# Stick-breaking attention on eight cores: one stream per slot, or one stream per operation with rings between them, and the last projection begun inside the last head

## The chip, the cores and the metric

The kernel runs on the 8 cores of one Trainium2 chip; each core works on one batch element, and no core talks to another. The metric is device time in microseconds (us) of the slowest core. Most executions of one kernel agree within about 0.3%, except for a second, slower state in which one die or both have a lower granted TensorE clock.

Engines are named as in the profile: PE is TensorE, DVE is VectorE, ACT is ScalarE, POOL is GpSimd, SP is SyncE (here it only issues DMAs). An engine runs its instructions in the order in which the program lists them (in the trace of the changed kernel POOL's 384 differences and SP's 256 transposes keep it).

## The reference

The model has one mLSTM layer and one stick-breaking attention layer, both with a projection in, a projection out and a LayerNorm. The change touches the second layer only:

```python
def _stick_breaking(q, k, v):                      # q,k,v: [B,16 heads,2048,128]
    ...
    for blk in range(s // QBLOCK):                 # blocks of 128 queries
        z = einsum(qb, kp) * scale                 # [.., 128, t1], keys up to t1
        mask = key < query
        log_1mb = where(mask, log_sigmoid(-z), 0)
        between = cumsum(log_1mb, reverse=True) - log_1mb
        a = where(mask, exp(log_sigmoid(z) + between), 0)
        outs.append(einsum(a, vp))

def _stick_breaking_layer(x, k_sh, v_sh, w_in, w_out, ln_g, ln_b):
    u = x @ w_in;  q, z = split(u)                 # k_sh, v_sh = split(x @ kv_w)
    att = _stick_breaking(q, k_sh, v_sh)
    y = (att * silu(z)) @ w_out
    return layernorm(ALPHA * x + y, ln_g, ln_b)
```

The kernel computes the running product R of sigmoid(-z) with a scan from the last key to the first; the attention weights are the differences of neighbouring values of R.

## The kernel before

The program is built by a small scheduler. Each activity is a Python generator that yields operations; the scheduler keeps an estimated time for each engine and each buffer, always takes the operation that could start first by that estimate, and so fixes the order of every engine's instructions when the program is built. I call these estimates its **beliefs**. On the chip, semaphores keep the results right whatever the real times are, but the order can't change any more.

```python
    def dma(self, q, slot, out, in_, R=(), W=(), A=(), cost=4.0, **kw):
        ...
        start = self.est(q, list(R) + list(A), W)
        ...
        self.t[q] = start + (1.0 if q == "pool" else 0.1)
        self.tdma = max(self.tdma, start) + cost      # ONE line of DMA work for all queues
        self._time(self.tdma + 2.0, R, W)             # believed landing
```

For each of 16 heads, 4 projections (K, Q, V and the gate; 64 matmuls of 512 columns each; each has 0.5 MB of weights, which come from HBM by POOL's queue into one of four buffers) run beside 16 query blocks of attention. One block was one sequential stream, and two such streams ran side by side:

```python
            def tblock(k, slot):
                ...
                chunks = [(0, n)] if n <= 8 else [(8, n), (0, 8)]       # n key blocks of 128
                for ci, (b0, b1) in enumerate(chunks):
                    yield lambda: any(zfree)                            # one of two PSUM regions of 1024
                    ... matmuls Q.K -> PZ[zi]                           # PE   "scores"
                    ... sigmoid(-scale * PZ[zi]) in place               # ACT
                    ... tensor_tensor_scan -> RR[slot]                  # DVE  "scan"
                    ... AA[slot] = RR shifted - RR                      # POOL "difference"
                yield DMA transpose AA[slot] -> TT[gi][:, 0:n, block j] # SP   "transpose"
            def av():  # per group of four blocks: TT[gi] x V -> PSUM, times gate, to DRAM "midd"
            ...
            Sched(kb).run([av(), counted(0), counted(1), loads(), proj()])
            kb.barrier()
            ... ln_epilogue(...)   # load midd, 16 tiles: 64 matmuls each, residual, LayerNorm, store
```

Of the kernel before, what the change touches and what calls it, by code (L numbers as in the profile page):

```python
# [15 lines left out]
KC = 16  # L16
# [9 lines left out]
class KB:  # L26
# [4 lines left out]
    def __init__(self, nc, es):  # L31
        self.nc = nc
        self.es = es
        self.eng = {"pe": nc.tensor, "act": nc.scalar, "dve": nc.vector, "pool": nc.gpsimd, "sp": nc.sync}
        self.sem = {e: es.enter_context(nc.semaphore("s_" + e)) for e in ("pe", "act", "dve", "pool")}
        self.cnt = {e: 0 for e in self.sem}
        self.seen = {e: {} for e in self.eng}
        self.lastw = {}
        self.reads = {}
        self.pend = {e: ([], []) for e in self.eng}  # L40
        self.dsem = {}
        self.semobj = dict(self.sem)
        self.t = {e: 0.0 for e in self.eng}
        self.tdma = 0.0
        self.tw = {}
        self.tr = {}
# [45 lines left out]
    def est(self, e, R, W):  # L92
        R, W = self._norm(R, W)
        t = self.t[e]
        for k in R:
            t = max(t, self.tw.get(k, 0.0))
        for k in W:
            t = max(t, self.tw.get(k, 0.0), self.tr.get(k, 0.0))
        return t

    def _time(self, end, R, W):
        for k in R:
            self.tr[k] = max(self.tr.get(k, 0.0), end)
        for k in W:
            self.tw[k] = end

    def op(self, e, fn, R=(), W=(), inc=True, cost=0.3):
# [12 lines left out]
        self._time(start + cost + self.LAT[e], R, W)  # L120
# [12 lines left out]
    def dma(self, q, slot, out, in_, R=(), W=(), A=(), cost=4.0, **kw):  # L133
# [8 lines left out]
        self.tdma = max(self.tdma, start) + cost  # L142
        self._time(self.tdma + 2.0, R, W)
# [25 lines left out]
class Sched:  # L169
# [6 lines left out]
    def run(self, streams):  # L176
        live = [[g, None] for g in streams]
        while live:
            best, bt = None, None
            for s in live:  # L180
                while s[1] is None:
                    try:
# [14 lines left out]
                t = self.kb.est(o.e, o.R, o.W)  # L197
                if o.slack and t > self.kb.t[o.e]:
                    t += o.slack
                if bt is None or t < bt - 1e-9:  # L200
                    best, bt = s, t
            ended = any(s[0] is None for s in live)
# [17 lines left out]
def build():  # L220
# [20 lines left out]
    with contextlib.ExitStack() as es:  # L241
# [3 lines left out]
        WB = [sb(f"WB{i}", [128, KC, 128], BF16) for i in range(2)]  # L245
# [603 lines left out]
        def phase_b(x_src, dst, SRC, skey):  # L849
# [4 lines left out]
            WS = WB + [sa(f"WBx{i}", [128, KC, 128], BF16) for i in range(2)]  # L854
            QTs = [sa(f"QTb{i}", [128, S], BF16) for i in range(2)]
            KTs = [sa(f"KTb{i}", [128, S], BF16) for i in range(2)]
            VVs = [sa(f"VVb{i}", [128, NT, 128], BF16) for i in range(2)]
            SZs = [sa(f"SZb{i}", [128, S], F32) for i in range(2)]
            VT = sa("VTb", [128, S], BF16)
            TZ = [sa(f"TZ{i}", [128, 512], F32) for i in range(2)]  # L860
            AA = [sa(f"AA{i}", [128, S], BF16) for i in range(2)]
            TT = [sa(f"TT{i}", [128, NT, 512], BF16) for i in range(2)]
            ST = [sa(f"ST{i}", [128, 512], BF16) for i in range(2)]
            MK = sa("MK", [128, 2048], BF16)
# [3 lines left out]
            kb.op("dve", lambda: V.memset(MK[:, 0:1920], 0.0), W=["MK"])  # L868
            kb.op("dve", lambda: V.tensor_scalar(out=MK[:, 1920:2048], in0=MASKL[:], scalar1=1.0, scalar2=None,
                                                 op0=ALU.mult), R=["MASKL"], W=["MK"])  # L870
            for i in range(2):
                kb.op("dve", lambda: V.memset(RR[i][:, 2048:2056], 1.0), W=[f"SCR{i}"])

            st = {"heads": -1, "tb": -1, "av": -1, "uload": 0, "uused": 0, "z": 0}
            zfree = [True, True]
            rfree = [True, True]
            PZ = [PSA[:, 0:1024], PSA[:, 1024:2048]]
            zkeys = [[("ps", 0), ("ps", 1)], [("ps", 2), ("ps", 3)]]
            BAV = [4, 5]
            BPJ = [6, 7]  # L880

# [4 lines left out]
            def loads():  # L886
                for i, (w, u) in enumerate(units):
                    while st["uused"] < i - 3:
                        yield lambda i=i: st["uused"] >= i - 3
                    yield Op("pool", None, W=[f"WB{i % 4}"], cost=5.0,  # L890
                             dma=dict(slot=f"wb{i % 4}", out=WS[i % 4][:], in_=w[u]))
                    st["uload"] = i + 1

            def proj():
                nbk = 0
                for i in range(len(units)):
                    h, kind = i // 4, i % 4
                    par = h % 2
                    if kind == 0:
                        yield lambda h=h: st["heads"] >= h - 2  # L900
                    yield lambda i=i: st["uload"] > i
                    for tb in range(4):
                        bank = BPJ[nbk % 2]
                        nbk += 1
                        tsl = slice(tb * 512, (tb + 1) * 512)
                        for c in range(KC):
                            yield Op("pe", lambda c=c, bank=bank, i=i, tsl=tsl: P_.matmul(  # L907
                                PS[bank], lhsT=WS[i % 4][:, c, :], rhs=SRC[:, c, tsl], start=(c == 0),
                                stop=(c == KC - 1)), R=[f"WB{i % 4}", skey], W=[("ps", bank)], inc=(c == KC - 1),
                                cost=0.216)  # L910
                        if kind == 3:
                            zi = nbk % 2
                            yield Op("act", lambda bank=bank, zi=zi: A_.activation(out=TZ[zi][:], in_=PS[bank],
                                                                                   func=AF.Sigmoid),
                                     R=[("ps", bank)], W=[f"TZ{zi}"], cost=0.65)
                            yield Op("dve", lambda bank=bank, zi=zi, tsl=tsl, par=par: V.tensor_tensor(
                                out=SZs[par][:, tsl], in0=PS[bank], in1=TZ[zi][:], op=ALU.mult),
                                R=[("ps", bank), f"TZ{zi}"], W=[("SZ", par, tb)], cost=0.7)
                        else:
                            dstT, key = ((KTs[par], ("KT", par)), (QTs[par], ("QT", par)), (VT, "VT"))[kind]  # L920
                            yield Op("act", lambda dstT=dstT, bank=bank, tsl=tsl: A_.copy(out=dstT[:, tsl],
                                                                                          in_=PS[bank]),
                                     R=[("ps", bank)], W=[key], cost=0.65)
                    st["uused"] = i + 1
                    if kind == 2:
                        yield Op("sp", None, R=["VT"], W=[("VV", par)], cost=2.5,
                                 dma=dict(slot=f"vv{par}", out=VVs[par][:], in_=VT[:], transpose=True))
                    if kind == 3:
                        st["proj"] = h
                for nb in range(4):  # L930
                    yield Op("pool", None, W=[skey], cost=11.0,
                             dma=dict(slot=f"wo{nb}", out=SRC[:, :, nb * 512:(nb + 1) * 512], in_=b_w_out[nb]))

            st["proj"] = -1
            blocks = [(h, gq, j) for h in range(NH_B) for gq in range(4) for j in range(4)]

            def tblock(k, slot):
                h, gq, j = blocks[k]
                par, gi = h % 2, (4 * h + gq) % 2
                tb = 4 * gq + j  # L940
                n = tb + 1
                off = S - 128 * n
                yield lambda: st["proj"] >= h
                yield lambda: st["av"] >= 4 * h + gq - 2
                chunks = [(0, n)] if n <= 8 else [(8, n), (0, 8)]
                for ci, (b0, b1) in enumerate(chunks):
                    w = (b1 - b0) * 128
                    zi = []
                    yield lambda: any(zfree)
                    zi = zfree.index(True)  # L950
                    zfree[zi] = False
                    for o in range(0, w, 512):
                        ww = min(512, w - o)
                        yield Op("pe", lambda zi=zi, o=o, ww=ww, b0=b0: P_.matmul(  # L954
                            PZ[zi][:, o:o + ww], lhsT=QTs[par][:, tb * 128:(tb + 1) * 128],
                            rhs=KTs[par][:, b0 * 128 + o:b0 * 128 + o + ww], start=True, stop=True),
                            R=[("KT", par), ("QT", par)], W=[zkeys[zi][o // 512]], cost=max(ww, 128) / 2400 + 0.01,
                            slack=0.5)
                    zk = zkeys[zi][:(w + 511) // 512]
                    yield Op("act", lambda zi=zi, w=w: A_.activation(out=PZ[zi][:, 0:w], in_=PZ[zi][:, 0:w],  # L960
                                                                     func=AF.Sigmoid, scale=-scale),
                             R=zk, W=zk, cost=0.2 + w * 0.000833)
                    mk = MK[:, 2048 - w:2048] if ci == 0 else MK[:, 0:w]
# [107 lines left out]
```

## Time and profile before

Median 3506 us; the traced execution took 3498.88 us, its slowest core 3497.3 us. The timeline has three stages: the mLSTM layer to 1548 us, the heads to 3225, the last projection with LayerNorm to 3497.

The view of windows gives the busy time of each engine in a stretch. After the stretch and its length come PE, PEld (weight loads), DVE, ACT and POOL, each with the number of instructions, then the granted TensorE clock (1.00 is full speed), the busy share of the DMA engines and GB/s. Before, slowest core:

```profile
2900.00:3000.00 100.00, 80.37 (x344) 33.72 (x343) 44.83 (x33) 28.03 (x42) 36.50 (x30) 0.91 0.47 77
3088.00:3225.00 137.00, 28.95 (x81) 8.47 (x79) 43.00 (x29) 18.48 (x26) 37.82 (x28) 0.55 0.63 98
3225.00:3245.00 20.00, 0.00 (x0) 0.00 (x0) 0.00 (x0) 1.12 (x1) 0.00 (x0) 0.50 0.89 280
3245.00:3497.00 252.00, 224.38 (x1024) 99.61 (x1024) 149.49 (x176) 6.49 (x32) 72.10 (x16) 0.97 0.44 153
```

In the heads (first row) no engine is full, and 80.37 overstates PE: a matmul that stands alone is shown with its whole latency, about 0.4 us, while 128 projection matmuls in a row take 27.8 us (0.217 us each). The last head (second row) is nearly a hole.

The view of waits, before, from the second to the fifteenth head (columns: who waited, for whom, us in total, times, longest):

```profile
POOL WBx L146 <- PE PSA L907: 210.1, 13, 17.0
PE PSA L954 <- DVE SCR L966: 134.0, 155, 3.2
POOL AA L971 <- DMA TT<-AA: 128.8, 61, 3.7
PE PSA L994 <- DMA TT<-AA: 127.2, 40, 5.2
```

L954 is scores, L966 scan, L971 difference, L994 AV. PE waits for scans and for transposes: 261 us in 13 heads, 20 us a head. POOL's wait in the first line is for a weight buffer that PE still reads.

The chain of waits in the last head, before (start, length, what): POOL's in-order queue stands behind the loads of the output weights (in the program all four loads write one key, so each waits until the one before has landed).

```profile
3088.80 17.53 DMA HT<-b_w_out
3106.99 17.75 DMA HT<-b_w_out
3125.38 18.96 DMA HT<-b_w_out
```

### The profile page before, as it was taken

The page shows a single profiled execution, that of the slowest core. Times are in us where ns is not written, and L with a number is a line of the kernel's source. Part 1 is how long each engine was busy: PE and PEld are TensorE (multiplying, and loading weights), DVE is VectorE, ACT ScalarE, POOL GpSimd, SP SyncE. Part 2 cuts the span into 40 slices and gives each one's busy share as a digit, 9 for nine tenths or more (in the row PEclk, how much of TensorE's full clock was granted, in tenths as well). Part 3 has the DMA queues.
Part 4 walks back from the last instruction along what each step waited for, and adds up shares of the span by engine and source line. Part 5 has one row for each costly group of instructions (what it writes and reads, how often), then busy time and mean ns, then how long its engine had stood idle before and what let it go on. Part 6 is the DMA issues. An engine that isn't in the chain of part 4 may idle for free.

```text
span 3497.3 us, 38611 instructions; the slowest of 8 cores (3480.0 to 3497.3 us)
## 1 busy us (share of the span) xinstructions
PE 2819.5 (81%) x13444; PEld 1285.7 (37%) x13444; DVE 1606.0 (46%) x2768; ACT 1084.5 (31%) x2016; POOL 923.8 (26%) x732
## 2 busy tenths in 40 slices
PE   5899999999999869978878877887877877832897
PEld 4344444444444324433333333333333333310343
DVE  2354454544544355533444444544444444513465
ACT  2253453544535422222222222322222222301000
POOL 0021220211212212222333333333333333313233
PEclk9999999999999969989999999999999999965999
DMA  8121202202112163333544444444444444364453
GB/s 228 21 37 19 37 13 49 37 13 43 33 23 37 23 146 128 138 98 67 77 75 81 79 74 83 79 71 80 82 73 80 78 78 81 70 95 96 166 184 131
DMA packets 387053, 271.09 MB, mean 78 GB/s; under 512 B 326864, under 2 KB 359728, under 8 KB 376112
## 3 DMA queue, kind: packets, MB, share of 16 engines
q1 hardware_dynamic: 349856, 184.65, 21.7%
q0 software_dynamic: 37008, 83.96, 15.3%
q8 instruction: 113, 1.85, 0.2%
q14 instruction: 76, 0.62, 0.1%
HBM read 230.88 MB, written 41.94 MB: 78 GB/s over the span
## 4 chain that ended last, share of the span: by engine, by line
PE 55%; DVE 14%; DMA 14%; POOL 6%; issue 5%; ACT 4%; SPq 1%; DVEq 0%; POOLq 0%; ACTq 0%
PE PSA L907 13%; PE PSA L651 12%; PE PSA L372 9%; DVE SCR L966 9%; DMA TT<-AA 8%; PE PSA L314 6%; PE PSA L548 6%; POOL AA L971 4%; PE PSA L994 3%; PE PSA L954 2%; DMA XT<-a_w_out 2%; ACT PSA L960 2%; DMA HT<-b_w_out 2%; POOL SCR L393 1%; DMA HT<-x 1%
## 5 line engine op out<-in xcount | busy, mean ns | idle before, releaser
L971 POOL TENSOR_TENSOR AA<-SCR 128x1024 bf16<-128x1024 f32 (+7 forms) x384 | 530.8, 1390 | 506.3 <-DVE SCR L966 332.2
L907 PE MATMUL PSA<-HT,WB 128*128 128x512 bf16 x2048 | 555.7, 399 | 8.8 <-DMA WB<-kv_w 8.8
L907 PE MATMUL PSA<-HT,WBx 128*128 128x512 bf16 x2048 | 505.1, 390 | 0.0
L651 PE MATMUL PSA<-XT,GW 128*128 128x512 bf16 x2048 | 477.2, 392 | 0.0
L960 ACT ACTIVATE PSA<-PSA 128x1024 f32<-128x1024 f32 (+7 forms) x384 | 287.6, 759 | 592.4 <-PE PSA L954 590.7
L966 DVE TENSOR_TENSOR_SCAN SCR<-PSA,MK 128x128 f32<-128x128 f32 (+7 forms) x256 | 340.1, 1348 | 236.0 <-ACT PSA L960 148.6
L994 PE MATMUL PSA<-TT,VVb 128*128 128x512 bf16 (+3 forms) x640 | 248.0, 397 | 180.7 <-DMA TT<-AA 179.8
L954 PE MATMUL PSA<-KTb,QTb 128*128 128x512 bf16 (+3 forms) x640 | 195.2, 373 | 230.3 <-DVE SCR L966 230.1
L966 DVE TENSOR_TENSOR_SCAN SCR<-PSA,SCR,MK 128x1024 f32<-128x1024 f32 x128 | 298.7, 2342 | 146.2 <-POOL AA L971 76.2
L907 PEld LDWEIGHTS PSA<-HT,WB 128*128 128x128 bf16 x2048 | 205.6, 102 | 250.2 <-issue 55.3
L907 PEld LDWEIGHTS PSA<-HT,WBx 128*128 128x128 bf16 x2048 | 204.5, 100 | 252.0 <-issue 28.0
L651 PEld LDWEIGHTS PSA<-XT,GW 128*128 128x128 bf16 x2048 | 205.6, 101 | 240.9 <-issue 29.2
L393 POOL TENSOR_TENSOR SCR<-SCR,LNG 128x2048 f32<-128x2048 f32 x32 | 144.2, 4508 | 412.8 <-DVE SCR L390 412.8
L372 PE MATMUL PSA<-HT,MG 128*128 128x512 bf16 x1024 | 224.4, 381 | 31.9 <-DMA MG<-midd 23.0
L548 PE MATMUL PSA<-XT,WB 128*128 128x512 bf16 x1024 | 235.0, 382 | 2.4 <-ACT DB L502 2.4
L372 PE MATMUL PSA<-XT,HT 128*128 128x512 bf16 x1024 | 225.4, 381 | 4.7 <-DMA XT<-a_w_out 4.7
L314 PE MATMUL PSA<-XT,WB 128*128 128x512 bf16 x1024 | 222.3, 379 | 0.0
L1000 DVE TENSOR_TENSOR ST<-PSA,SZb 128x512 bf16<-128x512 f32 x64 | 43.8, 685 | 342.6 <-PE PSA L994 342.6
L669 POOL TENSOR_TENSOR SCR<-SCR 128x512 f32<-128x512 f32 x64 | 81.0, 1265 | 416.7 <-ACT SCR L667 416.7
L954 PEld LDWEIGHTS PSA<-KTb,QTb 128*128 128x128 bf16 x640 | 54.3, 99 | 360.4 <-issue 337.4
L994 PEld LDWEIGHTS PSA<-TT,VVb 128*128 128x128 bf16 x640 | 68.3, 107 | 287.4 <-issue 241.7
L725 DVE SCALAR_TENSOR_TENSOR STM<-PSA,WW,MASKC 128x128 bf16<-128x128 f32 x128 | 44.9, 351 | 247.7 <-PE PSA L723 225.6
(145 smaller groups left out, 2846.8 us busy)
## 6 DMA issues: line engine op xcount, KB each, us to landing
y<-SCR SPq DMA_DIRECT2D x32, 1024.0 KB, 3.9
SCR<-x SPq DMA_DIRECT2D x24, 1024.0 KB, 5.2
WB<-a_w_in POOLq DMA_DIRECT2D x32, 512.0 KB, 5.2
GW<-a_w_in POOLq DMA_DIRECT2D x32, 512.0 KB, 11.5
SCR<-y SPq DMA_DIRECT2D x16, 1024.0 KB, 5.9
HT<-x SPq DMA_DIRECT2D x8, 1024.0 KB, 10.3
XT<-a_w_out POOLq DMA_DIRECT2D x4, 2048.0 KB, 15.2
WB<-kv_w POOLq DMA_DIRECT2D x16, 512.0 KB, 6.2
```

The costliest lines, as they stand in the source:

```text
L314: kb.op("pe", lambda: P_.matmul(PS[bank][:, :], lhsT=WB[u.slot][:, c, :], rhs=src[:, c, tb * 512:(tb + 1) * 512], start=(c == 0), stop=(c ...
L372: kb.op("pe", lambda: P_.matmul(PS[bank][:, :], lhsT=midf(c, t), rhs=wo_buf[:, c, nb * 512:(nb + 1) * 512], start=(c == 0), stop=(c == KC ...
L393: kb.op("pool", lambda: G.tensor_tensor(out=full, in0=full, in1=LNG[:], op=ALU.mult), R=[sk, "LNG"], W=[sk])
L548: kb.op("pe", lambda: P_.matmul(PS[bank][:, :], lhsT=WB[u.slot][:, c, :], rhs=XT[:, c, tb * 512:(tb + 1) * 512], start=(c == 0), stop=(c = ...
L651: kb.op("pe", lambda: P_.matmul(PS[gb_][:, :], lhsT=gw[:, c, :], rhs=XT[:, c, tb * 512:(tb + 1) * 512], start=(c == 0), stop=(c == KC - 1) ...
L669: kb.op("pool", lambda: G.tensor_tensor(out=GO[pp], in0=GO[pp], in1=GWf[pp], op=ALU.add), R=[ko, kw] + gco[pp] + gcw[pp], W=[ko])
L907: yield Op("pe", lambda c=c, bank=bank, i=i, tsl=tsl: P_.matmul(PS[bank], lhsT=WS[i % 4][:, c, :], rhs=SRC[:, c, tsl], start=(c == 0), sto ...
L954: yield Op("pe", lambda zi=zi, o=o, ww=ww, b0=b0: P_.matmul(PZ[zi][:, o:o + ww], lhsT=QTs[par][:, tb * 128:(tb + 1) * 128], rhs=KTs[par][: ...
L960: yield Op("act", lambda zi=zi, w=w: A_.activation(out=PZ[zi][:, 0:w], in_=PZ[zi][:, 0:w], func=AF.Sigmoid, scale=-scale), R=zk, W=zk, cos ...
L966: yield Op("dve", lambda zi=zi, w=w, mk=mk, lo=lo, hi=hi, init=init: V.tensor_tensor_scan(out=RR[slot][:, lo:hi][:, ::-1], data0=PZ[zi][:, ...
L971: yield Op("pool", lambda lo=lo, hi=hi, b0=b0, b1=b1: G.tensor_tensor(out=AA[slot][:, b0 * 128:b1 * 128], in0=RR[slot][:, lo + 1:hi + 1], ...
L994: yield Op("pe", lambda sb_=sb_, f0=f0, bank=bank, par=par, gi=gi, nb_=nb_: P_.matmul(PS[bank][:, f0:512], lhsT=VVs[par][:, sb_, :], rhs=T ...
```

## The change

The intent: no engine should wait for the latency of a single block. Every operation gets a stream of its own, with rings between: five PSUM banks of 512 columns for scores, a ring of 32 key blocks for differences, V transposed in quarters, output weights loaded per column block, and the last projection is a stream that may start while the last head still runs. The core of the diff (cut):

```diff
-        self.tdma = 0.0
+        self.tdma = {}
 ...
-        self.tdma = max(self.tdma, start) + cost
-        self._time(self.tdma + 2.0, R, W)
+        self.tdma[q] = max(self.tdma.get(q, 0.0), start) + cost
+        self._time(self.tdma[q] + 2.5, R, W)
 ...
-            def tblock(k, slot):  ... scores, sigmoid, scan, difference, transpose in one stream
+            def zs():             # for every block, chunks of 512 from the diagonal down
+                        bank = zfree.pop(0)
+                        ... matmul -> PS[bank]; sigmoid in place; zq.append((k, ci, bank))
+            def scan():           # cost=0.12 + w * 0.0022
+                        ... scan PS[bank] -> RR[slot]; zfree.append(bank); sq.append((k, ci))
+            def sub():            # ring AA of 32 blocks; waits for the transposes that still read its place
+                        ... difference of up to two chunks -> AA[pos ...]
+            def trn():            # cost=0.1 + n * 0.05 (was 0.3 + n * 0.15)
+                        ... DMA transpose AA -> TT[gi]
 ...
+            def outp():           # the last projection, tiles 0 to 3 column block by column block
+            def aux():            # loads of midd, residual tiles, LayerNorm parameters in the last head
+            def ln(par):          # LayerNorm of odd and even tiles
-            Sched(kb).run([av(), counted(0), counted(1), loads(), proj()])
+            Sched(kb).run([av(), trn(), sub(), scan(), zs(), loads(), ln(0), ln(1), proj(), outp(), aux(), mgl()])
```

The first six lines: the scheduler now believes that each issuing queue has a line of DMA work of its own. The diff changes the estimates in two more places: the delay between engines is added only where two different engines meet, and AV is placed as if its inputs came 3 us later (1 us before).

## The prediction

> **What bounds it now.** The timeline of the slowest core has three stages: mLSTM layer to 1548 us; stick-breaking heads to 3225; last projection with LayerNorm to 3497. The change touches the last two.
>
> In the heads no engine is full. Windows of 2900 to 3000: PE 80, DVE 45, POOL 37, ACT 28 busy of 100 us, granted clock 0.91, DMA 47%. PE busy overstates: 128 projection matmuls take 27.8 us (0.217 each), an isolated one shows 0.4. Issue-limited, PE needs 256 x 0.217 = 55.5 us of projection and 2 x 7.4 us of scores and AV per head: 70.4. The V transposes of successive heads are 98.4 us apart ((3074.8-1599.2)/15). So 28 us per head are latency. The view of waits (1620 to 3080): scores wait for scans 157 us, AV for transposes 147, POOL for transposes 155, scans for POOL 109 and ACT 187. One sequential stream per slot (scores, sigmoid, scan, difference, transpose), two PSUM regions and one difference buffer per slot put each block's latency onto the in-order PE.
>
> Last head: 3088 to 3225, 137 us with PE busy 29, clock 0.55; POOL sits behind the b_w_out loads (the chain has three pieces of 18 to 19 us on them). Then 20 us for the mid tile, and 252 us for 16 tiles (14.0 us of matmul each, pitch 14.8).
>
> **What the change does.** PE work is the same. Scans go from 24 to 40 per head: 43.9 us against 39.9 (estimate from 1.21 us for 512 columns, 0.05 more when chained); with SZ and ST DVE needs 50 to 54 us per head, POOL 35, ACT 30. All are below 70, so PE should become the limit. Five one-bank score buffers, a ring of 32 blocks of differences and finer transposes remove most scan, POOL and transpose waits. The b_w_out loads are split by column block, residual and LN parameters are prefetched, and four output tiles (56 us) fill the last head. Those gains are on the critical path; the extra scans are not.
>
> **Sum (estimate).** 1548 + 9 first weights + 889 projection + 237 scores and AV + 222 output projection + 10 last LN = 2915 with a full PE. I add 75 for stalls: the static order believes 1.25 us per scan where scan plus gap comes near 1.35 (about 4 us per head), and transposes land late beside weight loads (median 3.5, at most 14.6 us now). Predicted 2990 us, range 2925 to 3090. Faster by over 2%: 0.96; within 2%: 0.03; slower: 0.01.
>
> **What would show it.** Head pitch 71 to 78 us; granted clock above 0.97 there; DVE about 70%, DMA near 60%; scores' waits for scans below 60 us in total; no hole in the last head; output tiles at 14.0 us pitch, 12 of them after the last AV; stage one unchanged within 5 us.
>
> **What would make it wrong.** (1) The Trainium skill, "TensorE: Matmul & The Clock Gate", Part 1, says an idle array falls to half clock, which the 0.55 of the last head agrees with, and that dense matmuls on three cores of a die can bring a 13/16 limit. Stage one, dense at 0.97 to 1.00, doesn't show it in this run; the slow execution (3713) might. A denser heads stage could meet it oftener: then near 3150. (2) DMA: 46 us of queue time per head in a 72 us pitch; if transposes queue behind weight loads, AV stalls and the pitch stays at 80 or more. (3) SP's in-order queue (1.1 to 1.3 us per transpose) blocking.

## The result, and the profile after

| | before | after |
|---|---|---|
| median of all runs, us | 3506.01 | 3202.07 (3197.66 to 3211.72) |
| slowest core of the traced run, us | 3497.3 | 3196.2 |
| first weight load of a projection matmul on PE to the last, us | 1555.3 to 3087.6 | 1557.2 to 2929.0 |
| from there to the end, us | 409.7 | 267.2 |
| mean head pitch (V transposes, 2nd to 15th head), us | 98.5 | 86.7 |

Ratios are the mean time of one kernel's fast runs over that of the other's fast runs of the same rounds, so not quite the ratio of the medians quoted. Here the ratio is 0.9139, 95% interval 0.9113 to 0.9166. The change is clearly faster, but by 304 us, not by the 516 us predicted, and 3202 us lies far outside the range of 2925 to 3090.

Windows after, slowest core: a stretch of middle heads, the end of the last head, and the last projection.

```profile
2500.00:2600.00 100.00, 85.95 (x376) 38.21 (x382) 59.08 (x59) 33.46 (x65) 45.10 (x35) 0.93 0.49 90
2929.00:2987.00 58.00, 41.76 (x169) 17.20 (x169) 28.95 (x33) 8.71 (x17) 14.85 (x9) 0.85 0.78 169
2987.00:3196.00 209.00, 193.46 (x883) 87.95 (x899) 127.05 (x184) 34.36 (x19) 81.75 (x33) 0.97 0.50 177
```

The hole at the end is gone. The middle heads are not full: 382 matmul weight loads in 100 us, where run 5 below reaches 444.

Waits after, second to fifteenth head (L980 scores, L1007 scan, L1033 difference, L1064 AV, L149 is the line of all DMA issues):

```profile
POOL WSA L149 <- PE PSA L1064: 203.6, 13, 17.2
POOL AAb L1033 <- DMA TT<-AAb: 193.0, 27, 12.7
PE PSA L1064 <- DMA TT<-AAb: 92.8, 13, 12.0
PE PSA L980 <- DVE SCR L1007: 60.7, 41, 4.3
```

Compared with before, the many short waits are fewer, and a few long ones have appeared: AV now waits once per head, for 5 to 12 us, and differences wait for transposes up to 12.7 us for room in the ring. The waits of POOL and AV for transposes, which the rings were to remove, did not fall: 128.8 + 127.2 = 256 us before, 193.0 + 92.8 = 286 after. Where the expected gain went can be put in numbers, because the sum of the prediction can be read off the trace:

| term | predicted, us | trace of the change, us |
|---|---|---|
| to the first projection matmul | 1557 | 1557.2 |
| PE work (projections 889, scores and AV 237, output 222) | 1348 | same matmuls |
| stalls | 75 | 3180.9 - 1557.2 - 1348 = 276 |
| after the last matmul | 10 | 3196.2 - 3180.9 = 15 |

One term is wrong. About 206 of the 276 us are gaps of PE, summed over the trace. The remaining 70 are work at half clock: in the same stretch PE was busy for 139.5 us inside the trace's half-clock periods, work that takes half as long at full clock. Without these 70 us and the gaps the trace leaves 1348 us of work, as predicted (the same reckoning leaves 1369 in run 5 and 1357 in run 12, so it is good to some 20 us). The Trainium skill, "TensorE: Matmul & The Clock Gate", Part 1, says that the clock is halved after an idle window of about 3.4 us and comes back after a busy one; the trace agrees, its half-clock periods in the heads last 3.4, 6.8, 10.2 or 13.7 us and lie at the gaps.

One head of the trace shows where such a gap comes from. POOL's timeline after (start, us, what; in brackets the idle time before it and what ended it):

```profile
2345.13 0.57 POOL L149 DMA_DIRECT2D WSA<-kv_w  x1 [0.29 <-issue]
2355.72 7.21 POOL L1033 TENSOR_TENSOR AAb<-SCR 128x1024 bf16<-128x1024 f32 x4 [10.02 <-DMA TT<-AAb]
2362.89 0.57 POOL L149 DMA_DIRECT2D WSA<-b_w_in  x1
```

and the chain of waits after, in the same head:

```profile
2359.22 3.73 POOL AAb L1033 x2
...
2363.06 7.72 DMA TT<-AAb
2370.78 0.14 issue
2370.92 1.44 PE PSA L1064 x3
```

POOL issues a weight load at 2345.13. A transpose of 14 blocks is issued at 2345.84 and lands 9.8 us later, where the fastest transpose of that length took 4.2. POOL idles 10.0 us until the ring has room again. Then the same happens again: load at 2362.89, transpose at 2363.06, landing after 7.7 us, and AV, which the order has put in front of all further projection work, holds PE for 8.15 us. Summing the DMA packets of the trace per microsecond and queue shows why the transpose is late:

```
us       weights queue, KB   transposes' queue, KB
2346            33                 123
2347            98                   8
2348           156                   0
2349           156                   0
2350            45                 107
...
2364            70                   0
2365           152                   0
2366           176                   1
2367           123                  45
2368             4                 170
2369             0                 291
```

While a weight load flows, the transpose gets almost nothing. Of the 256 transposes of the heads, the 62 that were issued between the issue of a weight load and its landing landed after 7.03 us in the median, the other 194 after 3.54. Two run beside a load in every head, whichever was issued first: the second and the last block of the head's last group (14 and 16 key blocks), with 7.3 and 7.9 us in the median where the fastest took 4.2 and 4.3. AV of this group waits for the last one.

The scheduler can be asked at build time what it believed. It believed in a pitch of 71.9 us where the trace has 84 to 93. Lined up instruction by instruction, belief and trace part exactly at such transposes:

```
trace us   engine, what                      trace behind belief (since 2290), us
2322.13    POOL, weight load                 0.55
2323.78    SP, transpose, lands after 6.3    2.43
2329.13    POOL, difference (ring full)      4.93
2345.13    POOL, weight load                 3.26
2345.84    SP, transpose, lands after 9.8    5.45
2355.72    POOL, difference (ring full)     11.64
2370.89    PE, AV                           12.55
2379.47    POOL, difference (next head)     14.64
```

The 14 us lost in this head are about the whole difference between the believed pitch and the traced mean (86.7).

### The profile page after: what moved, and what is told of

Its sections match the earlier page's. It is cut to its first block, busy times and chain, and to the rows that moved or that the text cites. A ratio compares the mean times of both kernels' runs of the same rounds, so it can differ in the third digit from the quotient of the medians.

```text
span 3196.2 us, 39280 instructions; the slowest of 8 cores (3174.9 to 3196.2 us)
## 1 busy us (share of the span) xinstructions
PE 2747.7 (86%) x13190; PEld 1293.0 (40%) x13444; DVE 1637.3 (51%) x3046; ACT 1137.5 (36%) x2258; POOL 929.4 (29%) x749
## 3 DMA queue, kind: packets, MB, share of 16 engines
q1 hardware_dynamic: 351888, 184.66, 23.9%
q0 software_dynamic: 37008, 83.96, 17.6%
## 4 chain that ended last, share of the span: by engine, by line
PE 59%; issue 11%; DVE 10%; DMA 10%; POOL 6%; ACT 3%; SPq 1%; DVEq 0%; POOLq 0%; ACTq 0%
PE PSA L651 13%; PE PSA L918 11%; PE PSA L372 7%; PE PSA L314 7%; DVE SCR L1007 7%; PE PSA L548 6%; PE PSA L1113 6%; DMA TT<-AAb 6%; POOL AAb L1033 5%; PE PSA L1064 4%; DMA XT<-a_w_out 2%; DMA HT<-x 2%; PE PSA L980 1%; SPq L149 1%; PE PSA L804 1%
## 5 line engine op out<-in xcount | busy, mean ns | idle before, releaser
L918 PE MATMUL PSA<-HT,WSA 128*128 128x512 bf16 x4009 | 992.4, 387 | 15.5 <-DMA WSA<-kv_w 7.9
L1033 POOL TENSOR_TENSOR AAb<-SCR 128x1024 bf16<-128x1024 f32 (+7 forms) x384 | 526.5, 1389 | 550.9 <-DVE SCR L1007 294.6
L918 PEld LDWEIGHTS PSA<-HT,WSA 128*128 128x128 bf16 x4096 | 403.2, 99 | 481.5 <-issue 46.7
L985 ACT ACTIVATE PSA<-PSA 128x512 f32<-128x512 f32 (+3 forms) x640 | 325.6, 519 | 565.8 <-PE PSA L980 552.3
L1007 DVE TENSOR_TENSOR_SCAN SCR<-PSA,MK 128x512 f32<-128x512 f32 (+3 forms) x256 | 280.5, 1106 | 309.2 <-ACT PSA L985 157.8
L1007 DVE TENSOR_TENSOR_SCAN SCR<-PSA,SCR,MK 128x512 f32<-128x512 f32 (+3 forms) x384 | 415.6, 1082 | 41.8 <-DVE SCR L1007 9.7
L980 PE MATMUL PSA<-QK 128*128 128x512 bf16 (+3 forms) x631 | 218.0, 354 | 83.3 <-DVE SCR L1007 82.7
L1064 PE MATMUL PSA<-TT,VVb 128*128 128x512 bf16 (+3 forms) x628 | 161.8, 412 | 112.5 <-DMA TT<-AAb 111.5
L930 ACT CAST QK<-PSA 128x512 bf16<-128x512 f32 x128 | 75.3, 588 | 247.1 <-PE PSA L918 242.5
L1064 PEld LDWEIGHTS PSA<-TT,VVb 128*128 128x128 bf16 x640 | 69.7, 111 | 210.8 <-issue 163.4
L372 PEld LDWEIGHTS PSA<-XT,HT 128*128 128x128 bf16 x1024 | 100.2, 99 | 129.3 <-issue 13.7
L314 PEld LDWEIGHTS PSA<-XT,WB 128*128 128x128 bf16 x1024 | 100.3, 98 | 120.7
L526 DVE SCALAR_TENSOR_TENSOR SCR<-SCR,PRT 128x512 f32<-128x512 f32 x192 | 144.4, 752 | 6.8
L548 PEld LDWEIGHTS PSA<-XT,WB 128*128 128x128 bf16 x1024 | 100.2, 98 | 109.1 <-issue 5.2
L980 PEld LDWEIGHTS PSA<-QK 128*128 128x128 bf16 x640 | 63.2, 99 | 182.1 <-issue 127.3
## 6 DMA issues: line engine op xcount, KB each, us to landing
GW<-a_w_in POOLq DMA_DIRECT2D x32, 512.0 KB, 11.3
```

What stands on the lines that cost most here:

```text
L314: kb.op("pe", lambda: P_.matmul(PS[bank][:, :], lhsT=WB[u.slot][:, c, :], rhs=src[:, c, tb * 512:(tb + 1) * 512], start=(c == 0), stop=(c ...
L372: kb.op("pe", lambda: P_.matmul(PS[bank][:, :], lhsT=midf(c, t), rhs=wo_buf[:, c, nb * 512:(nb + 1) * 512], start=(c == 0), stop=(c == KC ...
L526: kb.op("dve", lambda: V.scalar_tensor_tensor(out=accb, in0=ub(k), scalar=wk(k), in1=accb, op0=ALU.mult, op1=ALU.add), R=ur + [("ACC", tb) ...
L548: kb.op("pe", lambda: P_.matmul(PS[bank][:, :], lhsT=WB[u.slot][:, c, :], rhs=XT[:, c, tb * 512:(tb + 1) * 512], start=(c == 0), stop=(c = ...
L918: yield Op("pe", lambda c=c: P_.matmul(PS[bank], lhsT=WS[i % 4][:, c, :], rhs=SRC[:, c, tsl], start=(c == 0), stop=(c == KC - 1)), R=[f"WB ...
L980: yield Op("pe", lambda: P_.matmul(PS[bank][:, 0:w], lhsT=QTs[par][:, (n - 1) * 128:n * 128], rhs=KTs[par][:, b0 * 128:b1 * 128], start=Tr ...
```

## The experiments

**Theory A.** Transposes stand behind weight loads in the DMA engines; the scheduler, which believes the queues independent, places AV and differences as if they landed in 3 us, and the fixed order passes the delay on to PE. **Rival B.** POOL stands 16 us a head in front of a weight load, waiting for PE (first line of the waits), and with it the differences. **Rival C.** The prediction's own: scans take longer than believed. Each edit is against the changed kernel. The sets 1 to 4, 5 to 8, 9 to 11 and 12 to 14 each shared a chip and the runs of the kernel before. Pitch and PE's idle time per head are read from the traces between the 2nd and 15th V transpose; for the change they are 86.7 and 12.1 us. Where AV stands in PE's order is read from the kernels, built again with the order written out; it is the same in all the middle heads of a run.

### 1. A quarter of the weight bytes (wrong result)

```diff
-  dma=dict(slot=f"wb{i % 4}", out=WS[i % 4], in_=w[u])
+  kc = KC if i < 4 else KC // 4
+  dma=dict(slot=f"wb{i % 4}", out=WS[i % 4][:, 0:kc, :], in_=w[u][:, 0:kc, :])
```

> Wrong result on purpose: from the fifth unit on, each weight load of the heads moves 4 of its 16 chunks; every engine's order, every wait and every load instruction stays. Theory A (transposes stand behind the 1 MB weight loads in the DMA engines, 4 us longer each time, about 14 us of drift a head): head pitch falls from 86 to 72-76 us, median time to 3010-3070 us. Rivals B (POOL stands 16 us a head in front of a weight load, waiting for PE) and C (scans slower than the scheduler believes): nothing they name is changed, so pitch stays 84-87 and time within 2% of 3202.

Measured: fast runs 3044.8 to 3052.0, ratio 0.8697; pitch 75.3, PE idle 3.3 us a head. Waits of this run:

```profile
POOL WSA L149 <- PE PSA L1065: 207.0, 13, 17.3
PE PSA L1065 <- DMA TT<-AAb: 15.0, 9, 2.7
```

About 152 us go with the bytes alone, and transposes that meet a load land after 4.05 us in the median, not 7.03. POOL's wait for PE, which B blames, is unchanged at 207 us. The cause passes through the DMA. (A load is 0.5 MB; the 1 MB of the expectation is a slip.)

### 2. Weight loads one unit later in POOL's queue

```diff
-  yield lambda i=i: st["uused"] >= i - 3
+  yield lambda i=i: st["uused"] >= (i - 2 if 3 < i < 60 else i - 3)
```

> Each weight load is put one unit (14 us) later in POOL's queue, so POOL no longer waits for PE there; orders of PE, DVE, ACT and SP are the same, bytes the same. Rival B: POOL's 236 us of waits before weight loads fall below 40 us and the time falls by 100 to 200 us, to 3000-3100. Theory A: loads only meet other transposes; POOL's waits before loads vanish too, but time stays within 60 us of 3202.

Measured: fast runs 3129.9 to 3149.2, ratio 0.8952; pitch 81.4. That is 70 us faster, between the two expectations, and a little more than A allowed. The waits of this run:

```profile
POOL AAb L1033 <- DMA TT<-AAb: 352.6, 28, 20.6
PE PSA L1064 <- DMA TT<-AAb: 84.9, 13, 8.3
```

B's wait is gone (0.3 us left), yet AV waits for transposes nearly as long as in the change (84.9 against 92.8 us). Only 31 transposes now meet a load, not 62. The gain fits loads that meet fewer transposes; POOL's standing before a load is not the main cost. This run alone leaves room for a share of B; runs 5 and 12 take it up again.

### 3. The scheduler is told of longer scans

```diff
-  cost=0.12 + w * 0.0022)
+  cost=0.22 + w * 0.0022)
```

> The scheduler is told 0.10 us more for each scan, nothing else. The prediction's own term, rival C (real scans and gaps longer than believed cost 4 us a head): pitch falls by 3 to 5 us, time to 3130-3155. Theory A: within 1% of 3202.

Measured: two fast runs (3131.8 and 3157.6; two slow), ratio 0.8977; pitch 80.7. This is C's number, and a miss for A. But the waits don't fit C's reason:

```profile
PE PSA L980 <- DVE SCR L1007: 60.1, 38, 4.5
PE PSA L1064 <- DMA TT<-AAb: 25.5, 7, 6.5
```

Scores wait for scans as long as in the change (60.1 against 60.7 us); what fell is AV's wait for transposes, from 92.8 to 25.5. AV itself has not moved: the last AV of a head stands two projection matmuls and one score earlier in PE's order than in the change. The transpose that it waits for meets a load less often: it landed in under 5 us in six of the 13 heads, and AV waited in the other seven; in the change it took 7.6 us or more in all 13. So the gain fits A again, by a shift in time and not by a better order. Run 9 tests whether scans have a share.

### 4. The scheduler is told that all transposes land 3 us later

```diff
-  self._time(self.tdma[q] + 2.5, R, W)
+  self._time(self.tdma[q] + (5.5 if kw.get("transpose") else 2.5), R, W)
```

> The scheduler is told that every transpose lands 3 us later than it was told (fixed part 5.5 in place of 2.5 us), so AV, scores and differences are ordered for late landings; bytes and buffers the same. Theory A with the order at fault: PE's waits for transposes fall from 111 us to below 40 and the pitch to 77-81, time to 3060-3130. If the ring of 32 blocks and the two AV buffers are at fault and not the order: waits for the ring remain and the time stays above 3150. Rivals B and C: no change over 1%.

Measured: fast runs 3113.0 to 3115.4, ratio 0.8892; pitch 81.1. In the traced stretch AV no longer waits for transposes at all (no such line), but scores wait 90.3 us for scans and differences 315.3 us for the ring. As expected by A in time (the pitch lies at the edge of 77 to 81). The last AV stands 49 projection matmuls and 7 scores later than in the change. Why this order is slower than the next run's is not shown.

### 5. One line of DMA work again in the belief

This undoes the first lines of the diff, except that the fixed part of a landing stays at 2.5 us (2.0 before).

```diff
-  self.tdma[q] = max(self.tdma.get(q, 0.0), start) + cost
-  self._time(self.tdma[q] + 2.5, R, W)
+  self.tdma["all"] = max(self.tdma.get("all", 0.0), start) + cost
+  self._time(self.tdma["all"] + 2.5, R, W)
```

> Undoes one part of the change: the scheduler again believes that all queues share one line of DMA work, so a transpose issued just after a weight load is believed to land up to 4 us later; bytes, buffers and kinds of instructions the same. Believed pitch 73.9 us (it was 71.9). Theory A (late transposes, known or unknown to the order): pitch 76-81 us, time 3040-3120. If the order plays no part: within 1% of 3202.

Measured: fast runs 3052.6 to 3066.5, ratio 0.8715; pitch 76.0, PE idle 3.8 us a head.

```profile
POOL WSA L149 <- PE PSA L1064: 206.0, 13, 17.2
PE PSA L980 <- DVE SCR L1007: 45.9, 60, 1.1
PE PSA L1064 <- DMA TT<-AAb: 3.1, 6, 1.3
```

Window of this run, to be held against the first row of the windows after:

```profile
2500.00:2600.00 100.00, 94.40 (x446) 41.99 (x444) 67.96 (x69) 41.37 (x82) 52.89 (x44) 1.00 0.66 110
```

AV's wait falls from 92.8 to 3.1 us, PE does 444 weight loads in 100 us in place of 382, and the clock is full. The DMA engines are busier than in the change (0.66 against 0.49), and even more transposes meet a load (100 against 62) and land nearly as late (6.71 us in the median). What moved is AV: the last one of a head stands 30 projection matmuls and 5 scores later in PE's order. At 0.217 us each that is 7.6 us (an estimate from the rate of the dense projections), about the 7.1 us a head that AV had waited. Late landings by themselves cost almost nothing when the order expects them, and DMA capacity is not the limit. B's wait is whole (206.0 us), and some 145 us are gone all the same.

### 6. Weight loads in four quarters

```diff
-  yield Op("pool", None, W=[f"WB{i % 4}"], cost=4.0, dma=... whole unit)
+  for p in range(4):          # one with each quarter of the projection of unit i - 3
+      yield lambda i=i, p=p: i < 4 or i == 63 or st["uq"] >= 4 * (i - 3) + p
+      yield Op("pool", None, W=[("WB", i % 4, p)], cost=1.0, dma=... chunks 4p to 4p+3)
```

> Each weight load goes out as four quarters, one with each quarter of the projection of the unit three before; bytes the same, 12 more POOL issues a head, POOL does not wait for PE long. Theory A: a transpose stands behind 1 to 1.5 us of weights in place of 4 to 6, mean landing falls from 4.9 to below 4.2 us, pitch to 75-79, time to 3030-3090. If only the sum of bytes counts (DMA bandwidth, 55% busy): pitch stays at 81 or more as in the late gate run, time 3125 or more.

Measured: two fast runs (3148.0 and 3181.6; two slow), ratio 0.9019; pitch 82.4. My expectation missed. Each collision did become cheaper (4.52 us in the median beside a load), but 158 transposes in place of 62 met one, and the order knew of none: AV still waited 47.7 us for transposes in 13 heads. This also fits the alternative named there, that only the sum of bytes counts; run 5, which has the same bytes per head, speaks against it.

### 7. Quarters and nearer beliefs

Runs 6 and 3 together, and `+ (4.5 if kw.get("transpose") else 2.5)` as in run 4.

> Quarters, and beliefs nearer the trace (scan 0.10 us longer, transposes 2 us later; believed pitch 75.3). Both measures work on the same late landings, so gains do not add: pitch 75-78, time 3020-3080, within 30 us of the quarters alone.

Measured: fast runs 3073.6 and 3083.3 (three slow, no ratio made); pitch 79.0, PE idle 5.2 us a head. The pitch lies just above the expected range, and the time is 65 to 108 us below the quarters alone, not within 30, so the nearer beliefs take most of it off. What the quarters add to them is not shown: these beliefs were not run without quarters.

### 8. No output tile before the last AV

```diff
-  yield lambda t=t, nb=nb: st["wo"] >= nb and st["mg"] >= 0 and st["x"] >= t
+  yield lambda t=t, nb=nb: (st["wo"] >= nb and st["mg"] >= 0 and st["x"] >= t
+                            and st["heads"] >= LAST)
```

> The change without its second half: no output tile before the last AV; everything else, the prefetched loads too, the same. The traced change has 1.9 of 16 tiles (26 us of PE) before the last AV, not 4, so the loss is 15 to 35 us: 3217 to 3237. The prediction (56 us of tiles in the last head) would have 45 to 60.

Measured: fast runs 3216.2 to 3231.3, ratio 0.9184; the mean is 19 us above the change, by the two ratios 16 us. The 95% intervals overlap (0.9133 to 0.9235 and 0.9113 to 0.9166), so the gain from tiles begun inside the last head is not clear of the noise; its size fits the 1.9 tiles of the trace (26 us).

### 9. One-DMA belief and longer believed scans

Run 5 with the edit of run 3.

> The one-DMA belief of the fifth run (3061 us) with the longer scan belief of the third. Rival C (scans longer than believed cost 4 us a head of their own): scores' waits for scans (3.5 us a head there) vanish and the time falls by 40 to 60 us, to 3000-3020. Theory A (the third run gained because any delay put AV later, behind the late transposes): nothing is left to gain there, within 20 us of 3061.

Measured: fast runs 3065.8 and 3074.5 (two slow), ratio 0.8769; pitch 77.1; scores wait 3.8 us a head for scans (3.5 in run 5). Nothing was left for C to gain. The scan belief in run 3 had worked through the transposes that no longer met a load.

### 10. Fewer loads ahead of the last transposes

```diff
   yield lambda: st["proj"] >= LAST
-  ... load LayerNorm gain; residual tiles 0 to 3
+  ... residual tiles 0, 1
+  yield lambda: st["tb"] >= len(blocks) - 1      # all transposes issued
+  ... residual tiles 2, 3; LayerNorm gain        # and tiles 0, 1 of all column blocks first
```

with the belief of run 5.

> The one-DMA belief, and in the last head only two residual tiles are loaded before the last transpose is issued; LayerNorm gain and two more tiles come after it. In the fifth run's trace a transpose of the last head stands behind five 1 MB loads of its own queue (landing up to 21.7 us), PE waits 11.6 us for it and then runs at half clock for 27 us. Gain 15 to 30 us: 3031 to 3046. No gain would mean that the last head is bound by scans.

Measured: fast runs 3054.9 and 3058.5 (two slow, no ratio made). A miss: within 1% of run 5. AV's longest wait for a transpose in the last head fell from 11.6 to 5.2 us, but scores wait for scans as before (16.0 us from 2650 us on; 17.6 in run 5), a half-clock period of 23.9 us remains (27.3 in run 5), and a new wait of 3.2 us has come in an output tile. That scans bound the last head fits this; no run took their waits away.

### 11. One-DMA belief and late loads

Runs 5 and 2 together.

> The one-DMA belief with weight loads one unit later in POOL's queue. Rival B (POOL standing 16 us a head before a load is a cost of its own): time falls by 40 to 70 us more, to 2990-3020. Theory A: POOL's wait was part of the order all along; time within 25 us of 3061, POOL's waits before loads gone.

Measured: fast runs 3126.9 to 3130.6, ratio 0.8937; pitch 81.7. Wrong for both: B expected a gain, A no loss.

```profile
POOL AAb L1033 <- DMA TT<-AAb: 368.2, 30, 20.6
PE PSA L1064 <- DMA TT<-AAb: 89.0, 13, 10.0
```

This is no new test of B: with late loads the shared belief changed almost nothing, PE's order is that of run 2 through the first 14 heads, and the time is run 2's too. What bounds B is run 5, which keeps its wait and lies within 1% of run 12, which has lost it. AV waits as in the change. The scheduler books DMA work in the order in which it takes operations. Twice a head it took a transpose just before a weight load, with the load's issue done 0.7 us **later**, and so believed in no meeting; on the chip the two transposes were issued 1.0 and 0.2 us **behind** the loads and landed after 8.4 and 7.9 us (medians). The shared line of DMA work is only a belief; nothing enforces it, and a margin of less than a microsecond was lost.

### 12. The believed order enforced

Run 11, and every load also waits for the landing of the newest transpose placed before it. The wait also enters the scheduler's estimate, so the order changes with it.

```diff
-  yield Op("pool", None, W=[f"WB{i % 4}"], cost=4.0, ...)
+  yield Op("pool", None, R=[st["newest"]], W=[f"WB{i % 4}"], cost=4.0, ...)
   ...
   st["tb"] = k
+  st["newest"] = ("TT", gi, j)
```

> The shared belief and late loads of the last run (3130 us, pitch 81.7), and each load also waits for the landing of the newest transpose put before it in the order, so that load and transpose cannot change places. Believed pitch 71.7. If the wrong order at the DMA engines is the cause: PE's waits for transposes fall from 6.8 to below 1.5 us a head, pitch to 73-77, time to 3010-3070. If the belief of the fifth run helped by accident: 3110-3150.

Measured: fast runs 3047.4, 3048.2, 3048.6 and 3076.2, correct, ratio 0.8722 (0.8672 to 0.8773); pitch 75.5, PE idle 3.2 us a head. Waits of this run:

```profile
POOL AAb L1034 <- DMA TT<-AAb: 316.3, 28, 18.9
POOL WSA L149 <- DMA TT<-AAb: 43.1, 11, 5.7
PE PSA L1066 <- DMA TT<-AAb: 5.5, 6, 1.9
```

and its window:

```profile
2500.00:2600.00 100.00, 94.29 (x433) 42.34 (x432) 68.39 (x68) 39.85 (x78) 48.53 (x40) 0.97 0.67 110
```

The edit makes the kernel about 80 us faster: AV's wait falls from 89.0 to 5.5 us, for one added wait (43 us of POOL's time in 13 heads). It works in two ways. Of the two transposes that had met a load in every head, the first now comes before it and lands after 4.0 us, not 8.4: that is the enforced order. The last one is still issued 0.3 us behind a load and lands after 8.0 us, but the order now expects it: AV stands 14 projection matmuls and 4 scores later than in run 11, about 3.9 us (18 x 0.217, an estimate). No run separates the two. Differences still wait for the ring 316 us, and it does no harm; POOL has the time.

### 13 and 14. Traced lengths of transposes in the belief

`cost=0.1 + n * 0.13` in place of `0.1 + n * 0.05`, in run 12 (13) and in run 5 (14).

> As the first, and the scheduler is told the traced length of transposes (0.13 in place of 0.05 us a block). Believed pitch 73.3. If order is the cause and lengths matter little: within 25 us of the first; if late landings by 1 to 1.3 us still hurt there, 15 to 40 us faster than it.

> The fifth run (3061 us) with the traced length of transposes, loads as in the change. Believed pitch 72.7 (73.9 there). Order the cause: 3020-3070. A time above 3100 would say that the fifth run's gain was luck of one order.

Measured: 13 has fast runs 3049.7 to 3054.9 (three slow), ratio 0.8715, pitch 75.1; 14 has 3052.3 to 3072.2 (one slow), ratio 0.8748, pitch 76.1. Both within what A expected. The gain of run 5 is not the luck of one order: four orders that know of the collisions (5, 12, 13, 14) lie within about 1% of each other.

## Why the prediction was wrong

- **Right:** what bounded the kernel before (latency of single blocks on the in-order PE), as far as its waits tell; the work terms, 1557 us measured and 1348 us as what gaps and half clock leave; that the extra scans cost little (scores' waits for scans fell from 134.0 to 60.7 us in 13 heads); the first stage unchanged (1555.3 and 1557.2 us to the first projection matmul).
- **Wrong, and the step that failed:** "I add 75 for stalls". The trace has 276. The prediction made this term of "about 4 us per head" for scans that take longer than believed, and of transposes that "land late beside weight loads". Run 9 gives the first part nothing of its own. The second is most of it: without the weight bytes 3050 us and 127 us of stalls (run 1), with an order that expects late transposes 3055 and 3048 us in the median of the fast runs and 133 and 124 us of stalls (runs 5 and 12). So about 145 to 150 of the 201 us of excess are late transposes that the order did not expect. A step before it failed with it: "finer transposes remove most scan, POOL and transpose waits" holds for scans, but the waits for transposes stayed (256 us before, 286 after; AV's part 127.2 and 92.8).
- **What stood in its place:** the rings remove the many short waits, but the change also told the scheduler that queues don't disturb each other. In the kernel before it believed one shared line of DMA work and in longer transposes; there the transposes that met a load landed after 4.2 us in the median (59 of 256). After the change, a weight load and a transpose met at the same two places in every head, and the meetings reached PE through the ring and AV (12 us idle a head) and then through the half clock.
- The risk "if transposes queue behind weight loads, AV stalls and the pitch stays at 80 or more" was named and came true (86.7 us), but for the wrong reason: I reckoned with DMA capacity (46 us of queue time in 72). Run 5 has the DMA busier and the pitch at 76.0. It was the order.
- "Granted clock above 0.97" (it was 0.93 from the second to the fifteenth head) and "12 tiles after the last AV" (14.1) failed as consequences. "Scores' waits for scans below 60 us in total" was nearly met (60.7 in 13 heads) and told nothing: the larger wait was AV's.
- Of the 301 us between the two traces, 160 come from the stretch of projections (mainly the pitch) and 142 from the last head and the projection behind it (409.7 to 267.2 us). Of that, begun tiles may give 16 to 20 us (run 8, not clear of the noise); the rest I put down to the output weights that no longer block POOL, to prefetched loads and to the tighter pitch of the tiles, without a run for each.
- **Open:** the same sum on run 12's trace leaves 3030.7 - 1558.8 - 1348 = 124 us of stalls, of which 57 are scores waiting for scans, in all heads, and 23 AV waiting for transposes, 17 of them in the last two heads; 31 us are work at half clock, reckoned as above. No run took these away.

## What to carry to other kernels

A static order is only as good as its model of shared resources. Here DMA queues that are issued separately shared the engines, and a load of 0.5 MB made a transpose beside it land 3.5 us later (7.03 against 3.54). Put such a dependence into the scheduler's belief, and where the believed margin is around a microsecond, enforce it with a real wait, as run 12 did on an engine with time to spare. Then look where the waiting instruction went in the order: an unchanged order (run 11) tests nothing. When you predict for a statically ordered program, look up in its cost model what it takes to be independent, and check that against the trace before you count the stalls.

## What the Trainium skill lacked or had wrong

- "DMA: Bandwidth & Descriptors", "Queues, rings and completion order": the page says that a DMA engine takes turns between its queues packet by packet, a packet being some 9 to 17 descriptors. It doesn't say what that means when packets differ in size. Here the trace's records of weights (4096 bytes, 324 ns in the median) and of transposes (256 bytes, 18 ns) shared engines; an estimate from taking turns record by record is 16 x 256 bytes per 342 ns, 12 KB per us for the transposes. In the 87 microseconds of 13 heads in which weights moved over 100 KB while a transpose was waiting (issued 2 us before or more, not landing within 0.5 us), transposes moved 11.3 KB in the mean and 6.1 in the median; alone they moved up to 291. So turns by single records fit the mean; which records form a packet of the page the trace doesn't show. No run changed the size apart from other things; in run 6, with records of 1024 bytes and 98 ns, the same estimate gives 35 KB, and the trace has 45.1 in the mean and 29.7 in the median (33 microseconds), but loads were also quarters.
- "TensorE: Matmul & The Clock Gate", Part 1: the page advises to reckon with 13/16 of the clock for dense matmuls on all cores. Where the order left PE without gaps, the slowest core of fast traced runs, with all eight at the same work, had more in the middle heads (run 5: 1.00, run 12: 0.97); means below 0.91 on the slowest core, down to 0.77, appear only in the slow runs, which came and went with the same program. The traces of four runs do hold stretches at 0.8125, which is 13/16, of 142 to 324 us in sum: on cores 0 and 1 alone in runs 2 and 8 (from 2920 to 3010 us of run 2 core 0 had 0.81 and core 2 had 1.00), on 4 and 5 in run 14, on 0 to 3 in run 6. The other cores did the same work without them. That these stretches make the slow state is not shown. The page doesn't name such a change from run to run.
- No page gives the time of a transpose within SBUF by its length: here 2.3 us to landing at 3 blocks of 128x128 and 4.3 at 16 (fastest of each), about 0.15 us a block.
